# Low-order dense products in bfloat16, sums ordered by operand type, and value products of two heads side by side

## The chip, the core and the metric

The kernel runs on one core of one Trainium2 chip. The metric is the device time of one execution in microseconds, as the median of the runs. TensorE (PE) multiplies, with its weight loads shown apart as PEld; VectorE (DVE), ScalarE (ACT) and GpSimd (POOL) do the elementwise work; SyncE (SP) issues most transfers.

## What is computed

Two layers of a hybrid decoder over 528 tokens (16 learned ones and 512 given) of width 1024, in float32:

```python
for l in range(2):
    u = rmsnorm(h, norm_mix[l])
    proj = u @ w_in[l]                      # 3340 columns
    mix = concat(gated_deltanet(...), diff_attention(...), swa_sinks(...), mamba2_ssd(...))
    h = h + mix @ w_out[l]
    u = rmsnorm(h, norm_ffn[l])
    h = h + (swiglu(u) if l == 0 else moe_swiglu(u))   # dense 2816; top 2 of 8 experts, 3584
y = rmsnorm(h, norm_final)[16:]
```

## The kernel before, in words

Activations lie transposed: 128 features on the partitions, 8 feature blocks, 528 tokens in two halves of 264 columns. A float32 matrix product is made of three cheaper ones. `split` (L192) cuts a float32 tile `raw` in two: `hi` is raw cast to float32r on ACT, `lo` is raw minus hi, also float32r, on DVE, or on POOL where `eng` is 2. `mm3` (L198) then issues hi by hi, hi by low and low by hi into one PSUM bank, 128 by 128 weights against 264 columns each. So a sum over 8 feature blocks is 24 float32r products, and one over 4 blocks (the output projection) 12.

Four stages follow one another. **Mixers 0** (layer 0): `norm` makes `uh` and `ul`; six *early* sums (the small columns and two tiles of keys) run while norm still works; then 24 more weight tiles go through `proj`, each loaded by `loadw` one tile ahead (DMA into `wraw`, two buffers; ACT casts `wh`; POOL subtracts `wl`), each tile as two sums of 24 products in four pieces of 6. Between the pieces run the steps of the four token mixers. Their order on PE is written out by hand: `TURNS` is a string of letters, one per step, p for a piece of projection, x for differential attention, s for sliding window attention, a and b for DeltaNet, d for the state space mixer; each generator's `yield` ends a step. Last comes `outproj` in two halves of 8 tiles. **The dense FFN** of layer 0 (`ffn`): 22 blocks of hidden features, two weight tiles each, then 24 tiles on the way down, all through `mm3`. **Mixers 1** is mixers 0 for layer 1. **The experts** (`up`, `down`): 8 experts with float32r high products and bfloat16 low ones, grouped by type in `mm2`; nothing there is touched.

In differential attention (`diff`, L941), `pv` (L1015) transposes one head's weights (`aT`, and the first 16 keys into the bank of `dpo`), ends the step, and in the next step multiplies them with `V`: 64 output rows, thus half the array's columns, one head after the other. `swa` (L1038) does the same per group (`waT`, `wpo`). These operands are plain float32, and each such product appears as two PE instructions in the trace. All engines but PE take their order from the tile scheduler, and work through it in that order.

Of the kernel before, what the change touches and what calls it, by code (L numbers as in the profile page):

```python
# [181 lines left out]
class Trunk:  # L182
    def __init__(self, tc, A, out, dumps=None):
        self.tc, self.nc, self.A, self.out, self.dumps = tc, tc.nc, A, out, dumps or {}
        self.nlayers = LAYERS
        self.overflow = True

# [122 lines left out]

    def four(self, name, dt=F32):
        return self.eight(name, dt).rearrange("p a b -> p (a b)")[:, :4 * D].rearrange("p (a b) -> p a b", a=4)
# [10 lines left out]
    def norm(self, pool, hT, wcol, l, uh, ul, rsb, t0=0):  # L323
# [3 lines left out]
        for k in range(KT):  # L327
            u = self.ftile("u")
            nc.vector.tensor_scalar(out=u[:, t0:], in0=hT[:, k, t0:], scalar1=self.par[:, l, wcol + k:wcol + k + 1], scalar2=None, op0=ALU.mult)
            self.split(u[:, t0:], uh[:, k, t0:], ul[:, k, t0:])  # L330
# [17 lines left out]
    def _mixers(self, ctx, l, hT):  # L348
# [10 lines left out]
        ul = self.ul = self.eight("ul", F32R)  # L359
# [76 lines left out]
    def mixed(self, name, y):  # L436

        for i in range(2):
            self.dump(f"{name}{self.l}_{i}", y[:, i])
            self.split(y[:, i], self.uh[:, PLACE[name] + i], self.ul[:, PLACE[name] + i])  # L440


    def proj_k(self, k, wh, wl, ps, j):
        s = slice(j * HALF, (j + 1) * HALF)
        self.mm3(ps[:wh.shape[2], :HALF], wh[:, k], wl[:, k], self.uh[:, k, s], self.ul[:, k, s], k == 0, k == KT - 1)

    def proj(self, j, half):
# [3 lines left out]
        for i in range(2):  # L451
            ps = self.ppt("pp")
            for k in range(KT):
                self.proj_k(k, wh, wl, ps, i)
                if k % 2 and k < KT - 1:
                    yield
            half(i, slice(i * HALF, (i + 1) * HALF), ps[:, :HALF])
# [483 lines left out]
    def diff(self):  # L941
# [18 lines left out]
        prev = None  # L960
        for i in range(2):
            yield from self.wait(f"f{i}")
            for c, (t0, n) in reversed(list(enumerate(CH))):
# [16 lines left out]
                for q in range(2):  # L980
# [31 lines left out]
        yield from prev  # L1012
        yield from self.headnorm(self.ma, fq, 4, 1.0 / 64, [dw, dw])

    def pv(self, a, c, h):  # L1015

        nc, tp = self.nc, self.tp
        t0, n = CH[c]
        pt = self.ma("aT", [128, 4, 128])
        at = tp.tile([128, 4, 128], F32, tag="aT", name="aT")  # L1020
        for j in range(1, c + 1):
            nc.tensor.transpose(pt[:, j - 1, :n], a[:n, CH[j][0]:CH[j][0] + 128], self.ident[:n, :n])
        if c:
            nc.scalar.copy(at[:, :c, :n], pt[:, :c, :n])
        po = self.ma("dpo", [128, 2, 128])
        nc.tensor.transpose(po[:16, 1, :n], a[:n, 0:16], self.ident[:n, :n])
        a0 = tp.tile([16, 128], F32, tag="aT0", name="aT0", bufs=1)
        nc.vector.tensor_copy(a0[:, :n], po[:16, 1, :n])
        po = po[:, 0]
        yield  # L1030
        p, vcol = slice(64 * (h % 2), 64 * (h % 2) + 64), 64 * h
        self.mm(po[p, :n], self.V[:16, 0, vcol:vcol + 64], a0[:, :n], True, c == 0)
        for j in range(1, c + 1):
            self.mm(po[p, :n], self.V[:, j, vcol:vcol + 64], at[:, j - 1, :n], False, j == c)

        nc.scalar.copy(self.fqk[p, 0, h // 2, t0:t0 + n], po[p, :n])

    def swa(self):  # L1038
# [4 lines left out]
        for c, (t0, n) in enumerate(CH):  # L1043
# [32 lines left out]
            yield  # L1076
            for g in range(2):
                p = slice(64 * g, 64 * g + 64)
                e = ee[:, 2 * g:2 * g + 2]

                ops = [[], []]
                v = self.V[:, :, 256 + 64 * g:320 + 64 * g]
                if full:
                    pt = self.ma("waT", [128, 2, 2, 128])
                    at = tp.tile([128, 2, 2, 128], F32, tag="waT", name="waT", bufs=1)
                    for r in range(2):
                        for q, j in enumerate(full):
                            k0 = CH[j][0] - s0
                            nc.tensor.transpose(pt[:, r, q, :n], e[:n, r, k0:k0 + 128], self.ident[:n, :n])
                            ops[r].append((v[:, j], at[:, r, q, :n]))  # L1090
                    nc.scalar.copy(at[:, :, :len(full), :n], pt[:, :, :len(full), :n])
                po = self.ma("wpo", [128, 4, 128])
                if c < 2:
                    a0 = tp.tile([16, 2, 128], F32, tag="waT0", name="waT0", bufs=1)
                    for r in range(2):
                        nc.tensor.transpose(po[:16, 2 + r, :n], e[:n, r, 0:16], self.ident[:n, :n])
                        ops[r].append((v[:16, 0], a0[:, r, :n]))
                    nc.vector.tensor_copy(a0[:, :, :n], po[:16, 2:4, :n])
                yield
                for r in range(2):  # L1100
                    for q, (vv, aa) in enumerate(ops[r]):
                        self.mm(po[p, r, :n], vv, aa, q == 0, q == len(ops[r]) - 1)

                nc.scalar.copy(wq[p, :, ts], po[p, 0:2, :n])
                yield
        self.stage.add("sw")

    def outproj(self, half, hT=None):
# [34 lines left out]
        for d in range(KT):  # L1143
# [7 lines left out]
            for j in range(2):  # L1151
                s = slice(w0 + j * hn, w0 + (j + 1) * hn)
                ps = banks[d % len(banks)]("ops")
                for q, k in enumerate(OUTK[half]):
# [546 lines left out]
```

## Time and profile before

| | us |
|---|---|
| median of 3 runs | 2416.12 (2413.11 to 2421.19) |
| the profiled execution | 2410.97 |
| its span, first to last instruction | 2409.1 |
| PE busy | 2320.4 (96%) |
| DVE / ACT / POOL busy | 1690.4 / 1307.9 / 291.8 |

The span is the stretch that all views share; the profiled execution's own time is 1.9 us longer. A busy time is the union of an engine's instructions. Matmuls overlap, so the mean length of one (280 ns and more) is not its price; the distance between the starts of two is. The granted clock is the share of full speed (2.4 GHz) that TensorE was given; it is 2.4 or 1.2 GHz at any moment, and a stage shows the mean.

### The profile page before, as it was taken

How to read it: one execution, taken by the hardware profiler on the slowest of the kernel's cores; microseconds unless marked ns; L12 is line 12 of the kernel's file. 1: busy time of each engine (PE TensorE's matmuls, PEld its weight loads, DVE VectorE, ACT ScalarE, POOL GpSimd, SP SyncE). 2: the span in 40 equal slices, each digit the busy share in tenths (PEclk: the TensorE clock that was granted, in tenths of full speed). 3: DMA queues.
4: the chain of work that ended last, by engine and by line, in shares of the span. 5: the costliest groups of instructions: out<-in, count | busy, mean ns of one | idle time of the engine just before them, and what ended most of it. 6: DMA issues, size and time to landing. Idle time of an engine off the chain costs nothing. (4 is left out here: it accounts for less than half of the span.)

```text
span 2409.1 us, 52816 instructions
## 1 busy us (share of the span) xinstructions
PE 2320.4 (96%) x22285; PEld 2158.4 (90%) x22285; DVE 1690.4 (70%) x2674; ACT 1307.9 (54%) x2004; POOL 291.8 (12%) x186
## 2 busy tenths in 40 slices
PE   7999999999999999999998999999999999999996
PEld 6887778999999987777788999999999999999895
DVE  7655566644433467556555989899998989798896
ACT  4333344333321323334225979787887878676684
POOL 3210112211110022111131300000000000010000
PEclk9999999999999989999898999999999999999998
DMA  4110012222223311001025999989899888888692
GB/s 133 62 37 19 28 49 77 79 88 88 93 88 106 110 53 53 28 27 36 23 89 193 373 377 367 368 350 361 336 361 353 338 333 336 308 351 316 255 365 107
DMA packets 81619, 452.84 MB, mean 188 GB/s; under 512 B 12324, under 2 KB 13236, under 8 KB 38368
## 3 DMA queue, kind: packets, MB, share of 16 engines
q1 hardware_dynamic: 76720, 435.76, 48.7%
q0 software_dynamic: 4656, 13.64, 1.5%
q8 instruction: 177, 2.90, 0.5%
q14 instruction: 66, 0.54, 0.1%
HBM read 439.68 MB, written 9.70 MB: 187 GB/s over the span
## 5 line engine op out<-in xcount | busy, mean ns | idle before, releaser
L190 PE MATMUL gu<-xT,eh 128*128 128x256 f32 (+5 forms) x3584 | 516.1, 296 | 4.0 <-ACT eh L1620 2.3
L190 PEld LDWEIGHTS gu<-xT,eh 128*128 128x128 f32 x3584 | 469.3, 189 | 7.7 <-ACT eh L1620 3.9
L1625 DVE TENSOR_TENSOR el<-erx,eh 128x2048 bf16<-128x2048 f32 x192 | 437.7, 2291 | 40.8 <-ACT eh L1620 38.1
L1620 ACT CAST eh<-erx 128x2048 fp32r<-128x2048 f32 x192 | 365.1, 1909 | 70.5 <-PE gu L190 26.7
L1625 DVE TENSOR_TENSOR el<-er,eh 128x2048 bf16<-128x2048 f32 x144 | 329.7, 2292 | 46.7 <-ACT eh L1620 46.0
L190 PEld LDWEIGHTS <-el 128*128 128x128 bf16 x5376 | 323.5, 97 | 22.6 <-DVE el L1625 1.5
L1620 ACT CAST eh<-er 128x2048 fp32r<-128x2048 f32 x144 | 274.5, 1909 | 52.0 <-PE yacc L190 28.3
L195 ACT CAST wh<-wraw 128x1024 fp32r<-128x1024 f32 (+2 forms) x138 | 141.1, 1024 | 288.0 <-PE dn L190 93.2
L190 PE MATMUL pp<-uh,wh 128*128 128x264 f32 (+1 forms) x864 | 271.7, 315 | 13.5 <-ACT uh L195 7.2
L190 PE MATMUL yacc<-h,eh 128*128 128x256 f32 (+5 forms) x1792 | 259.6, 296 | 0.8 <-ACT eh L1620 0.4
L190 PE MATMUL gu<-xb,el 128*128 128x128 bf16 (+5 forms) x3584 | 256.1, 224 | 0.0
L190 PE MATMUL pp<-uh,wl 128*128 128x264 f32 (+1 forms) x864 | 252.0, 292 | 4.1 <-POOL wl L196 3.5
L190 PE MATMUL pp<-ul,wh 128*128 128x264 f32 (+1 forms) x864 | 252.0, 292 | 1.3 <-DVE ul L196 1.1
L196 POOL TENSOR_TENSOR wl<-wraw,wh 128x1024 fp32r<-128x1024 f32 x66 | 159.7, 2421 | 676.3 <-ACT wh L195 559.5
L190 PEld LDWEIGHTS yacc<-h,eh 128*128 128x128 f32 x1792 | 234.5, 189 | 2.4 <-DVE yT L1676 0.9
L190 PE MATMUL gu<-fuh,wh 128*128 128x264 f32 x704 | 201.9, 287 | 0.0
L190 PE MATMUL gu<-ful,wh 128*128 128x264 f32 x704 | 201.5, 286 | 0.0
L190 PE MATMUL gu<-fuh,wl 128*128 128x264 f32 x704 | 200.6, 285 | 0.0
L190 PEld LDWEIGHTS pp<-uh,wh 128*128 128x128 f32 (+1 forms) x864 | 165.8, 192 | 32.6 <-issue 11.1
L190 PEld LDWEIGHTS pp<-uh,wl 128*128 128x128 f32 (+1 forms) x864 | 165.7, 192 | 6.5 <-POOL wl L196 3.9
L190 PEld LDWEIGHTS pp<-ul,wh 128*128 128x128 f32 (+1 forms) x864 | 166.3, 193 | 3.1 <-DVE ul L196 2.0
L196 DVE TENSOR_TENSOR wl<-wraw,wh 128x1024 fp32r<-128x1024 f32 (+2 forms) x72 | 84.2, 1169 | 94.5 <-ACT wh L195 94.2
(393 smaller groups left out, 3974.1 us busy)
## 6 DMA issues: line engine op xcount, KB each, us to landing
erx<-in_m_gu_dram SPq DMA_DIRECT2D x128, 1024.0 KB, 6.8
er<-in_m_gu_dram SPq DMA_DIRECT2D x96, 1024.0 KB, 7.6
erx<-in_m_d_dram SPq DMA_DIRECT2D x64, 1024.0 KB, 6.9
er<-in_m_d_dram SPq DMA_DIRECT2D x48, 1024.0 KB, 7.6
wraw<-in_w_b_dram SPq DMA_DIRECT2D x52, 512.0 KB, 3.7
wraw<-in_f_gu_dram SPq DMA_DIRECT2D x44, 512.0 KB, 3.7
wraw<-in_w_o_dram SPq DMA_DIRECT2D x16, 512.0 KB, 3.7
wraw<-in_f_d_dram SPq DMA_DIRECT2D x16, 512.0 KB, 3.5
```

The costliest lines, as they stand in the source:

```text
L190: return self.nc.tensor.matmul(out, lhsT, rhs, start=start, stop=stop, skip_group_check=True, **kw)
L195: nc.scalar.copy(hi, raw)
L196: (nc.gpsimd if eng == 2 else nc.vector).tensor_tensor(out=lo, in0=raw, in1=hi, op=ALU.subtract)
L1620: self.lastact = nc.scalar.copy(wh, raw)
L1625: nc.vector.tensor_tensor(out=wl, in0=raw, in1=wh, op=ALU.subtract)
```

## The change

1. A split now yields three tiles: `hi` in float32r as before, `low[0]` = raw minus hi in bfloat16, and `low[1]` = raw cast to bfloat16, a second ACT pass over the same tile. The two bfloat16 tiles take the room of the one float32r tile. Each product hi by low becomes `low[1]` by `low[0]`: of three products per feature block, one stays float32r and two are bfloat16.
2. `mm3s` orders a sum by type: all its float32r products first, then all its bfloat16 ones, and the other way round in the next sum (`turn_hi`), so the type changes once per sum. `proj` still cuts a sum into four pieces of 6; the early sums are grouped per feature block.
3. `pv` waits for two heads and multiplies them by turns, each into its own half of one bank; `swa` does so for its two groups. The number of steps, and `TURNS`, stay as they are. The transposed first 16 keys go into the fourth slot of the `aT` bank (a bank of their own in the last chunk).

```diff
-    def split(self, raw, hi, lo, eng=0):
+    def split(self, raw, hi, low, eng=0):
         nc.scalar.copy(hi, raw)
-        (nc.gpsimd if eng == 2 else nc.vector).tensor_tensor(out=lo, in0=raw, in1=hi, op=ALU.subtract)
+        (nc.gpsimd if eng == 2 else nc.vector).tensor_tensor(out=low[0], in0=raw, in1=hi, op=ALU.subtract)
+        nc.scalar.copy(low[1], raw)

-    def mm3(self, out, ah, al, bh, bl, start, stop):
-        self.mm(out, ah, bh, start, False)
-        self.mm(out, ah, bl, False, False)
-        self.mm(out, al, bh, False, stop)
+    def mm3s(self, out, terms, first=True, last=True, n=0):
+        ops = [[(wh, xh) for wh, _, xh, _ in terms], [p for _, wl, _, xl in terms for p in ((wl[1], xl[0]), (wl[0], xl[1]))]]
+        ops = ops[self.turn_hi] + ops[1 - self.turn_hi]
+        self.turn_hi = 1 - self.turn_hi
+        for i, (w, x) in enumerate(ops):
+            self.mm(out, w, x, first and i == 0, last and i == len(ops) - 1)
+            if n and i % n == n - 1 and i < len(ops) - 1:
+                yield
...
+    def eightb(self, name):
+        return self.b8.tile([128, 2, KT, T], BF16, tag="b8", name=name)
...
-        ul = self.ul = self.eight("ul", F32R)
+        ul = self.ul = self.eightb("ul")
...
         for k in range(KT):
-            for (wh, wl), ps in zip(ahead, early):
-                for j in range(2):
-                    self.proj_k(k, wh, wl, ps[j], j)
+            for part in range(2):
+                for (wh, wl), ps in zip(ahead, early):
+                    for j in range(2):
+                        s, o = slice(j * HALF, (j + 1) * HALF), ps[j][:wh.shape[2], :HALF]
+                        if not part:
+                            self.mm(o, wh[:, k], uh[:, k, s], k == 0, False)
+                        else:
+                            for q in range(2):
+                                self.mm(o, wl[:, 1 - q, k], ul[:, q, k, s], False, k == KT - 1 and q == 1)
...
-            for k in range(KT):
-                self.proj_k(k, wh, wl, ps, i)
-                if k % 2 and k < KT - 1:
-                    yield
+            yield from self.mm3s(ps[:wh.shape[2], :HALF], [(wh[:, k], self.both(wl, k), self.uh[:, k, s], self.both(self.ul, k, s)) for k in range(KT)], n=6)
...
                     if prev:
-                        yield from prev
-                    prev = self.pv(e[:, 1], c, 2 * i + q)
+                        pair.append(self.turn(*prev))
+                        yield
+                        if len(pair) == 2:
+                            self.pv(pair)
+                            pair = []
+                    prev = e[:, 1], c, 2 * i + q
...
+    def pv(self, pair):
+        po = self.ma("dpo", [128, 128])
+        for j in [*range(1, c + 1), 0]:
+            for _, h, a0, at in pair:
+                p, v = slice(64 * (h % 2), 64 * (h % 2) + 64), slice(64 * h, 64 * h + 64)
+                if j:
+                    self.mm(po[p, :n], self.V[:, j, v], at[:, j - 1, :n], j == 1, False)
+                else:
+                    self.mm(po[p, :n], self.V[:16, 0, v], a0[:, :n], c == 0, True)
+        nc.scalar.copy(self.fqk[:, 0, h0 // 2, t0:t0 + n], po[:, :n])
...
+            po = self.ma("wpo", [128, 2, 128])
+            for r in range(2):
+                for q in range(len(ops[0][r])):
+                    for g in range(2):
+                        self.mm(po[64 * g:64 * g + 64, r, :n], *ops[g][r][q], q == 0, q == len(ops[g][r]) - 1)
+            nc.scalar.copy(wq[:, :, ts], po[:, :, :n])
...
-        wl = self.wp.tile([128, KT, 128], F32R, tag="wl", name="wl")
+        wl = self.wp.tile([128, 2, KT, 128], BF16, tag="wl", name="wl")
```

Where it moves instructions. On PE, in the steady dense FFN (`gu` are the gate and up sums, `fuh`, `ful` the split activations), before:

```order
L190 MATMUL gu_5734<-ful_5214,wh_5704 128x264
L190 MATMUL gu_5734<-fuh_5213,wl_5705 128x264
L190 MATMUL gu_5734<-fuh_5213,wh_5704 128x264
L190 MATMUL gu_5734<-ful_5214,wh_5704 128x264
L190 MATMUL gu_5734<-fuh_5213,wl_5705 128x264
L190 MATMUL gu_5765<-fuh_5213,wh_5760 128x264
```

and now, at the boundary of two sums:

```order
L191 LDWEIGHTS wl
L191 MATMUL gu<-ful,wl 128x264
L191 MATMUL gu<-fuh,wh 128x264 x16
L191 LDWEIGHTS wl
L191 MATMUL gu<-ful,wl 128x264
L191 LDWEIGHTS wl
L191 MATMUL gu<-ful,wl 128x264
```

The three kinds no longer alternate: 32 bfloat16 products (two sums' low parts, each with a weight load of its own in the list) stand between 16 float32r ones (two sums' high parts).

On PE, in mixers 0, at the first chunk of differential attention (`fe` the attention weights, `fs` the next scores, `kq` a DeltaNet product, `aT_…` the first 16 keys), before, for one head:

```order
L1022 MATMUL aT<-ident,fe 128x128 x4
L1026 MATMUL dpo<-ident,fe 16x128
...
L190 MATMUL dpo<-aT_1266,V 64x128
L190 MATMUL dpo<-aT,V 64x128 x4
L190 MATMUL fs<-fqk 128x400 x2
```

and now, for the second head and then both:

```order
L1050 MATMUL aT<-ident,fe 128x128 x4
L1052 MATMUL aT_1445<-ident,fe 16x128
...
L191 MATMUL kq<-kbq,knqv 128x256 x4
L191 MATMUL dpo<-aT,V 64x128 x8
L191 MATMUL dpo<-aT_1279,V 64x128
L191 MATMUL dpo<-aT_1439,V 64x128
L191 MATMUL fs<-fqk 128x400 x2
```

The first head's products have moved behind the second head's transposes, and the ten products of two heads stand in one block, head by turn with head.

On ACT, in mixers 0, a little later (`fe` the exponentials of the scores, `dD` those of DeltaNet's decays, `fqk` the copy out of `dpo`), before:

```order
L195 CAST wh<-wraw 128x1024
L677 ACTIVATE dD<-lp,ngc 128x128 x4
L1024 COPY aT<-aT 128x512
L677 ACTIVATE dD<-lp,ngc 16x16 x4
L1036 COPY fqk<-dpo 64x128
L997 ACTIVATE fe,fsm<-fs,fmx 128x400
L195 CAST wh<-wraw 128x1024
```

and now:

```order
L198 CAST wl<-wraw 128x1024
L1026 ACTIVATE fe<-fe,frr 128x400
L196 CAST wh<-wraw 128x1024
L698 ACTIVATE dD<-lp,ngc 128x128 x4
L1054 COPY aT<-aT 128x512
L698 ACTIVATE dD<-lp,ngc 16x16 x4
L1072 COPY fqk<-dpo 128x128
L198 CAST wl<-wraw 128x1024
```

For each weight tile there is a second pass, `wl<-wraw`, and it stands in the same queue, between the same links of the mixers' chains; there are half as many copies out of `dpo`, of twice the rows.

## Rows read from the trace of the kernel before

**Rows 1.** The page: span, and busy time and instructions of each engine.
```profile
span 2409.1 us, 52816 instructions
PE 2320.4 (96%) x22285; PEld 2158.4 (90%) x22285; DVE 1690.4 (70%) x2674; ACT 1307.9 (54%) x2004; POOL 291.8 (12%) x186
```

**Rows 2.** Busy time by stage: mixers 0, dense FFN, mixers 1, experts.
```profile
core 0: us, PE busy (x) PEld busy (x) DVE busy (x) ACT busy (x) POOL busy (x), PEclk, DMA share, GB/s
0.00:442.60 442.60, 412.06 (x3992) 349.97 (x3992) 285.83 (x756) 169.34 (x417) 92.39 (x46) 0.98 0.18 59
442.60:833.50 390.90, 390.75 (x3187) 390.01 (x3186) 155.35 (x253) 108.34 (x169) 48.10 (x44) 0.99 0.30 92
833.50:1309.00 475.50, 442.43 (x4110) 378.99 (x4108) 277.34 (x772) 171.51 (x409) 92.18 (x46) 0.95 0.16 54
1309.00:2409.00 1100.00, 1075.17 (x11000) 1039.46 (x11000) 971.86 (x895) 858.71 (x1011) 59.11 (x50) 0.99 0.86 332
```

**Rows 3.** Groups of PE instructions, 500 to 700 us (steady dense FFN).
```profile
...
L190 PE MATMUL gu<-fuh,wl 128*128 128x264 f32 x548 | 155.3, 283 | 0.0
```

**Rows 4.** Timeline of PE in mixers 0: start, length in us, instruction.
```profile
...
414.02 0.28 PE L190 MATMUL ops<-uh,wl 128*128 128x264 f32 x1
414.24 0.51 PE L190 MATMUL fps<-rw,selb 12*128 12x264 bf16 x3
414.67 0.39 PE L190 MATMUL ops<-uh,wh 128*128 128x264 f32 x1
414.90 0.28 PE L190 MATMUL ops<-ul,wh 128*128 128x264 f32 x1
```

**Rows 5.** The same, where two bf16 forms follow each other.
```profile
...
123.77 0.40 PE L190 MATMUL fps<-rw,selb 48*128 48x264 bf16 x2
124.10 0.39 PE L190 MATMUL lp<-cb,identb 128*128 128x512 bf16 x1
```

**Rows 6.** Timeline of PE in the expert stage, three groups in a row.
```profile
...
1599.81 2.20 PE L190 MATMUL gu<-xT,eh 128*128 128x264 f32 x16
1601.85 1.09 PE L190 MATMUL gu<-xb,el 128*128 128x132 bf16 x16
1602.75 0.49 PE L190 MATMUL gu<-xT,eh 128*128 128x264 f32 x2
```

**Rows 7.** Groups of PE instructions: one kind of dense product per stage, of three.
```profile
...
L190 PE MATMUL pp<-uh,wl 128*128 128x264 f32 (+1 forms) x864 | 252.0, 292 | 4.1 <-POOL wl L196 3.5 <-DVE wl L196 0.6
...
L190 PE MATMUL gu<-fuh,wl 128*128 128x264 f32 x704 | 200.6, 285 | 0.0
...
L190 PE MATMUL dn<-hh,wl 128*128 128x264 f32 x352 | 99.9, 284 | 0.0
...
L190 PE MATMUL ops<-uh,wl 128*128 128x264 f32 (+1 forms) x256 | 72.9, 285 | 0.0
```

**Rows 8.** The same view, products of half the array's columns in two mixers.
```profile
...
L190 PE MATMUL dpo<-aT,V 128*64 128x128 f32 (+2 forms) x232 | 38.8, 293 | 4.5 <-DVE aT L1028 4.5
...
L190 PE MATMUL wpo<-waT,V 128*64 128x128 f32 (+2 forms) x136 | 19.9, 278 | 0.8 <-ACT waT L1091 0.7
```

**Rows 9.** Timeline of PE: half-array products of one head, then of four heads.
```profile
344.06 1.23 PE L190 MATMUL dpo<-aT,V 16*64 16x128 f32 x8 [0.37 <-DVE aT L1028]
...
355.12 0.45 PE L190 MATMUL sy<-sG,xd 128*64 128x128 f32 x4
...
355.82 0.44 PE L190 MATMUL sy<-sCE,sH 128*64 128x128 f32 x4
356.19 0.44 PE L1022 MATMUL aT<-ident,fe 128*128 128x128 f32 x2
```

**Rows 10.** Groups of ACT instructions, 0 to 1309 us: the casts of the splits.
```profile
...
L195 ACT CAST wh<-wraw 128x1024 fp32r<-128x1024 f32 (+2 forms) x138 | 141.1, 1024 | 288.0 <-PE dn L190 93.2 <-PE gu L190 87.4 <-PE pp L190 60.6
...
L195 ACT CAST uh<-u 128x528 fp32r<-128x528 f32 x16 | 9.4, 628 | 5.8 <-DVE u L329 5.8
```

**Rows 11.** What PE waited for, 0 to 1309 us: total us, times, longest.
```profile
...
PE pp L190 <- ACT uh L195: 7.2, 2, 6.9
```

More of the change, by code (lines that the diff above doesn't have):

```diff
@@ L186, in __init__, with mm3 @@
         self.overflow = True
+        self.turn_hi = 0
     def mm(self, out, lhsT, rhs, start, stop, **kw):
         return self.nc.tensor.matmul(out, lhsT, rhs, start=start, stop=stop, skip_group_check=True, **kw)
-    def split(self, raw, hi, lo, eng=0):
+    def split(self, raw, hi, low, eng=0):
         nc = self.nc
         nc.scalar.copy(hi, raw)
-        (nc.gpsimd if eng == 2 else nc.vector).tensor_tensor(out=lo, in0=raw, in1=hi, op=ALU.subtract)
-    def mm3(self, out, ah, al, bh, bl, start, stop):
-        self.mm(out, ah, bh, start, False)
-        self.mm(out, ah, bl, False, False)
-        self.mm(out, al, bh, False, stop)
+        (nc.gpsimd if eng == 2 else nc.vector).tensor_tensor(out=low[0], in0=raw, in1=hi, op=ALU.subtract)
+        nc.scalar.copy(low[1], raw)
+    def mm3(self, out, terms, first=True, last=True):
+        for _ in self.mm3s(out, terms, first, last):
+            pass
+    def mm3s(self, out, terms, first=True, last=True, n=0):
[6 more added lines that the diff above has]
+                yield
     def sums(self, ps_, src, mat, R, scale, pool):
@@ L439, in mixed @@
             self.dump(f"{name}{self.l}_{i}", y[:, i])
[L440 to L445, printed above, removed]
+            self.split(y[:, i], self.uh[:, PLACE[name] + i], self.both(self.ul, PLACE[name] + i))
     def proj(self, j, half):
@@ L959, in diff @@
         fq, fk = self.fqk[:, 0], self.fqk[:, 1]
-        prev = None
+        prev, pair = None, []
         for i in range(2):
@@ L1008, in diff @@
                     if prev:
-                        yield from prev
-                    prev = self.pv(e[:, 1], c, 2 * i + q)
+                        pair.append(self.turn(*prev))
[4 more added lines that the diff above has]
+                    prev = e[:, 1], c, 2 * i + q
         yield
-        yield from prev
+        pair.append(self.turn(*prev))
+        yield
+        self.pv(pair)
@@ L1023, in pv @@
         if c:
             nc.scalar.copy(at[:, :c, :n], pt[:, :c, :n])
[L1025 to L1032, printed above, removed]
@@ L1033, in pv @@
-        for j in range(1, c + 1):
-            self.mm(po[p, :n], self.V[:, j, vcol:vcol + 64], at[:, j - 1, :n], False, j == c)
-        nc.scalar.copy(self.fqk[p, 0, h // 2, t0:t0 + n], po[p, :n])
+        nc.vector.tensor_copy(a0[:, :n], p0[:, :n])
+        return c, h, a0, at
+    def pv(self, pair):
+        nc = self.nc
+        c, h0 = pair[0][:2]
+        t0, n = CH[c]
+        po = self.ma("dpo", [128, 128])
[7 more added lines that the diff above has]
+        nc.scalar.copy(self.fqk[:, 0, h0 // 2, t0:t0 + n], po[:, :n])
@@ L1076, in swa @@
             yield
+            ops = [[[], []], [[], []]]
             for g in range(2):
-                p = slice(64 * g, 64 * g + 64)
                 e = ee[:, 2 * g:2 * g + 2]
-                ops = [[], []]
                 v = self.V[:, :, 256 + 64 * g:320 + 64 * g]
-                if full:
[L1084 to L1090, printed above, removed]
+                pt = self.ma("waT", [128, 2, 2, 128])
+                at = tp.tile([128, 2, 2, 128], F32, tag="waT", name="waT", bufs=2)
+                for r in range(2):
+                    for q, j in enumerate(full):
+                        k0 = CH[j][0] - s0
+                        nc.tensor.transpose(pt[:, r, q, :n], e[:n, r, k0:k0 + 128], self.ident[:n, :n])
+                        ops[g][r].append((v[:, j], at[:, r, q, :n]))
+                    if c < 2:
+                        nc.tensor.transpose(pt[:16, r, 1, :n], e[:n, r, 0:16], self.ident[:n, :n])
+                        ops[g][r].append((v[:16, 0], at[:16, r, 1, :n]))
+                if full:
@@ L1091, in swa @@
                     nc.scalar.copy(at[:, :, :len(full), :n], pt[:, :, :len(full), :n])
-                po = self.ma("wpo", [128, 4, 128])
                 if c < 2:
[L1094 to L1098, printed above, removed]
@@ L1099, in swa @@
-                yield
[L1100 to L1105, printed above, removed]
+                    nc.vector.tensor_copy(at[:16, :, 1, :n], pt[:16, :, 1, :n])
+                yield
+            yield
+            po = self.ma("wpo", [128, 2, 128])
+            for r in range(2):
+                for q in range(len(ops[0][r])):
+                    for g in range(2):
+                        self.mm(po[64 * g:64 * g + 64, r, :n], *ops[g][r][q], q == 0, q == len(ops[g][r]) - 1)
```

35 lines of the change are left out of this document (20 added, 15 removed).

## The prediction

> **What bounds the kernel now.** I read the page first: PE is busy 96% of the span, DVE 70%, ACT 54% [rows 1]. Then the stages, since that mean hides their limits [rows 2]. In the dense FFN (442.6 to 833.5 us) PE is busy 390.75 of 390.90 us, DVE 155 and ACT 108: it lasts as long as its matmuls. In the two mixer stages PE is busy 412 of 442.6 us and 442 of 475.5 us; the 64 us left are waits in chains that run through DVE and ACT, so matmul time saved there comes out only where no chain takes over. The experts (1100 us) are untouched and end what went before, so I count them as unchanged.
>
> The trace counts the dense float32r products by kind: 864 `pp`, 704 `gu`, 352 `dn`, 256 `ops` of one kind, and as many of the two others [rows 7]. Two of three kinds become bfloat16: 2 × 1056 = 2112 in the FFN, 2 × 1120 = 2240 in the mixers, 4352 in all. The sums are 88 + 48 in the FFN (44 tiles up, 24 down, two halves each) and 108 + 64 in the mixers: 308, each with one change of type.
>
> **1. The price of a product.** In steady FFN, 200 us hold 548 float32r products of 264 columns of one kind [rows 3] and 547 of each of the two others, 1642 in all: 121.8 ns each. At 2.4 GHz the 264 columns alone take 110, so at most 12 ns can be won. The nearest bfloat16 rows are two. In the experts, 16 bfloat16 products of 132 columns fill the 0.90 us from 1601.85 to 1602.75 [rows 6]: 56 ns, so 112.5 ns for 264 columns. In mixers 0, three `fps` products of 264 columns span 0.51 us from first start to last end, and their float32r neighbour lasts 0.28 alone [rows 4]: (0.51 − 0.28) / 2 = 115 ns. I take 113, nearer the long steady rows with full weights; ends 112.5 and 115. That saves 8.8 ns (6.8 to 9.3): 18.6 us in the FFN, 19.7 us in the mixers. There the granted clock averages 0.98 and 0.95 [rows 2], which makes about 7% of the time half speed; in that, 264 columns take 220 ns in either type, so I count 18.3.
>
> The Trainium skill, "TensorE: Matmul & The Clock Gate", section on the back-to-back issue gap, gives N/2.4 + 2.5 ns for a warm matmul, with no operand type in it: 112.5 ns at 264 columns. The float32r row (121.8 ns) differs from it, so the row decides; taken for bfloat16 alone it would save 40 us before deductions, where I have 38.
>
> **2. Changes of type.** In the experts, 16 float32r products of 264 columns take 2.04 us up to the first bfloat16 one [rows 6], against 16 × 0.1218 = 1.95: a pair of changes costs 0.09 us there. Here the float32r weights after the last bfloat16 product load beside a product twice as long, so I take half, 0.023 us per change; ends 0 and 0.045. That is 136 × 0.023 = 3.1 us in the FFN and 172 × 0.023 = 4.0 in the mixers.
>
> **3. Two heads side by side.** `dpo` takes 38.8 us for 232 instructions, `wpo` 19.9 for 136 [rows 8]: 58.7 us, all in the mixers, one half of the array idle. What it costs when four heads' products lie in both halves, `sy` shows: 16 instructions, in four groups of 4, between 355.12 and the start of the next work at 356.19 [rows 9]: 67 ns each with the change-over, against 167 for `dpo` (38.8 / 232). At 67 the saving is 58.7 − 368 × 0.067 = 34 us; mere halving gives 29; with a quarter of that lost to groups too short to overlap (the 16-token chunk, two products) 22. I take halving less the half-speed share, 27.
>
> **4. What it adds.** ACT gets 138 further passes over weight tiles at 1.02 us [rows 10] and as many further passes over activations as there are splits. In the FFN that is 68 × 1.0 = 70 us plus some 25 on activations, on top of 108 busy of 391: hidden; if the cover were gone it would show as PE waiting for `wl`. In the mixers it is 70 × 1.02 = 72 us plus 32 passes of 0.63 [rows 10] = 20: 92 us on top of 341 busy of 918 [rows 2]. They stand in ACT's queue between links of the chains; what that costs I put into the share below. Plainly exposed is only the start of a stage, where PE follows `norm` block by block: before, PE waited 7.2 us for `uh` casts, in two places [rows 11]. Eight further passes of 0.63 us in each of three norms are 15 us of ACT time; PE's own work per block (18 products, 2.2 us) covers most, so 3 us; ends 0 and 9. The bfloat16 subtraction writes fewer bytes from the same inputs, and I leave it at its price; weight tiles come a tile ahead, and POOL is busy 92 us per mixer stage [rows 2]. No transfer is added; a `wraw` buffer is held one pass longer, which the tile of lead time covers. The `dpo` copies halve in number.
>
> **Which share comes out.** FFN: 18.6 − 3.1 = 15.5 us, all of it. Mixers: 18.3 − 4.0 + 27 = 41.3 us of PE time; I take three quarters, 31, because PE already stands for 64 of 918 us at ends of chains, where shorter filling work only lengthens the wait, and because the added ACT passes delay some links; ends one half and all. Sum: 15.5 + 31 − 3 = 43.5 us. The profiled execution took 2411.0 us, which gives 2367.5. The median of the runs stands 5 us above it; from there the forecast is 2416 − 43.5 = **2372.5 us**.
>
> **The rivals.**
> *A. A change of type is dear.* Where `fps` (bfloat16) stands between float32r products, the start before it is 0.22 us off instead of 0.12, the one after it about 0.20 instead of 0.11, and the next 0.23 instead of 0.12 [rows 4]: 0.29 us per pair, 0.145 per change. If type alone did that, 308 changes would cost 45 us, and products and changes together would lose 8 us (45 − 36.9). With 27 × 0.75 = 20 from the pairs and 3 lost at the starts: 9 us faster, 2407. Against it: `fps` uses 12 or 48 of 128 rows, and where bfloat16 `fps` is followed by bfloat16 `lp` on 128 rows the gap is the same 0.21 us (second start at 123.77 + 0.40 − 0.28, next at 124.10) [rows 5]; and the experts' change costs 0.045 [rows 6]. So the shape does it. The Trainium skill, "TensorEngine Tiling (Array Packing)", section on key properties, says that changing the tiling mode drains the engine; it does not name the type, and these rows agree.
> *B. The chains hold the mixers.* Only a quarter of the 41.3 us comes out: 15.5 + 10 − 3 = 22.5 us, 2394. For it: chains through DVE and ACT already end 64 us of waits. Against: DVE is busy 60% in the mixers, and most of PE's pieces there are filling work.
> *C. Slower: ACT's queue.* The 92 us of extra passes in the mixers delay exponentials and copies that PE waits for. It decides once 47% of them (43.5 / 92) reach PE's path; at three quarters, 69 us, the time is 2416 − 43.5 + 69 = 2441. For it: the passes stand directly ahead of such links, in order. Against: ACT is idle six tenths of these stages, and in 918 us the longest wait of PE for a cast is 6.9 us, at the very start [rows 11].
> *D. More than forecast.* All of the mixers' 41.3 us comes out, `sy`'s price holds for the pairs (34), changes cost nothing: 18.6 + 18.3 + 34 − 3 = 68 us, 2348.
> That the change does not do what it says is excluded by the instruction order: the products, types and pairs stand there as told.
>
> **How the numbers follow.** Chances: forecast 0.58, A 0.10, B 0.17, C 0.05, D 0.10. The low ends together (115 ns, 0.045 per change, half of the mixers with pairs at 22, 9 us at the starts) leave (14.4 − 6.1) + (14.2 − 7.7 + 22) / 2 − 9 = 13.5 us, 2402; the high ends are D. So 2348 to 2402 holds the forecast, B and half of D, about 0.8. A measurement of this kernel tells 0.3% (7 us) from no change. Faster by more: forecast, B, D and part of A, 0.87; within: the rest of A and a C that just cancels the gain, 0.08; slower: C, 0.05.
>
> **What would show it.** In the changed kernel's profile: the FFN some 375 us long, with bfloat16 products 113 ns apart; `dpo` and `wpo` together near 30 us busy; ACT some 185 us busier before the experts, PE's waits for ACT little longer; both mixer stages 12 to 18 us shorter; the experts within 3 us of 1100. Step 1 is wrong if steady bfloat16 products stand 118 ns or more apart; 2 if the gap at a change of type reaches 0.2 us; 3 if `dpo` stays above 25 us; the share, if the mixers shrink by less than 20 us together. The whole is wrong if the time is above 2402.

## The result, and the profile after

The changed kernel took 2380.68 us in the median of 4 runs (2376.56 to 2388.00), the kernel before, beside it, 2416.40 (4 runs): ratio 0.983, 95% interval 0.980 to 0.986, 36 us less. The forecast was 2372.5 in a range of 2348 to 2402. The profiled execution took 2376.56 us, 34.4 less than that of before.

The page of the changed kernel, against [rows 1]:

```profile
span 2374.8 us, 53054 instructions
PE 2268.1 (96%) x22285; PEld 2023.3 (85%) x22285; DVE 1689.6 (71%) x2674; ACT 1461.9 (62%) x2199; POOL 290.3 (12%) x186
```

PE is busy 52 us less for as many instructions, ACT 154 us more. Then the four stages, cut at the same first instructions as [rows 2] (columns as there):

```profile
0.00:427.50 427.50, 389.87 (x3993) 306.94 (x3993) 284.83 (x755) 208.32 (x460) 89.38 (x46) 0.98 0.19 60
427.50:805.10 377.60, 374.44 (x3188) 337.90 (x3187) 157.04 (x254) 192.74 (x292) 49.82 (x45) 0.98 0.31 97
805.10:1275.70 470.60, 429.72 (x4110) 339.44 (x4107) 276.39 (x773) 202.44 (x439) 91.17 (x46) 0.92 0.17 56
1275.70:2374.80 1099.10, 1074.05 (x11000) 1038.98 (x11000) 971.32 (x895) 858.41 (x1011) 59.96 (x50) 0.99 0.86 332
```

Mixers 0 are 15.1 us shorter, the FFN 13.3, mixers 1 only 4.9, the experts 0.9. The two mixer stages got the same edits; what differs is the granted clock of mixers 1, 0.92 where it was 0.95.

The price of products, by the timeline of steady FFN (start, length in us):

```profile
565.06 2.19 PE L191 MATMUL gu<-fuh,wh 128*128 128x264 f32 x16
567.09 3.77 PE L191 MATMUL gu<-ful,wl 128*128 128x264 bf16 x32
570.62 2.18 PE L191 MATMUL gu<-fuh,wh 128*128 128x264 f32 x16
```

From 565.06 to 570.62, 5.56 us, stand 16 float32r and 32 bfloat16 products and two changes of type. At 121.8 and 112.5 ns the products alone make 5.55: a change costs about 5 ns, an estimate from the last digit.

The pairs (groups of PE instructions) against [rows 8], and ACT's second passes over weight tiles against the first ones in [rows 10]:

```profile
L191 PE MATMUL dpo<-aT,V 128*64 128x128 f32 (+2 forms) x232 | 21.7, 297 | 1.8 <-DVE aT L1055 1.8
L191 PE MATMUL wpo<-waT,V 128*64 128x128 f32 (+2 forms) x136 | 10.0, 279 | 0.0
```

```profile
L198 ACT CAST wl<-wraw 128x1024 bf16<-128x1024 f32 (+2 forms) x138 | 140.8, 1022 | 178.1 <-PE dn L191 65.0 <-issue 39.1 <-PE pp L191 28.0
```

dpo and wpo take 31.7 us where they took 58.7. The second pass costs ACT what the first does, 1022 ns a tile against 1024.

Where the mixers' gain went shows best in one stretch of mixers 1: DeltaNet's last two scans, from `pS` to the last `po`, with the same products in both kernels. Busy time by stretch, before and after:

```profile
1156.50:1165.60 9.10, 9.10 (x73) 6.01 (x72) 3.69 (x6) 2.35 (x6) 0.67 (x1) 1.00 0.20 59
```

```profile
1117.20:1131.90 14.70, 14.70 (x72) 8.53 (x71) 2.09 (x5) 2.35 (x6) 0.00 (x0) 0.54 0.09 32
```

73 and 72 PE instructions, busy throughout, in 9.1 us at full clock and in 14.7 us at 0.54 of it. Up to the experts the records put TensorE at 1.2 GHz for 72 us before and 110 after, of them 48 and 76 in mixers 1 and 5 and 14 in the FFN. PE also waits a little more: the waits view to 1320 us sums to 65 us before and 81 after.

### The profile page after: what moved, and what is told of

It reads as the page before. It is cut to its first block, busy times and chain, and to the rows that moved or that the text cites. A ratio compares the mean times of both kernels' runs of the same rounds, so it can differ in the third digit from the quotient of the medians.

```text
span 2374.8 us, 53054 instructions
## 1 busy us (share of the span) xinstructions
PE 2268.1 (96%) x22285; PEld 2023.3 (85%) x22285; DVE 1689.6 (71%) x2674; ACT 1461.9 (62%) x2199; POOL 290.3 (12%) x186
## 5 line engine op out<-in xcount | busy, mean ns | idle before, releaser
L191 PEld LDWEIGHTS <-wl 128*128 128x128 bf16 (+1 forms) x4352 | 412.8, 100 | 100.1 <-issue 20.4
L191 PE MATMUL pp<-ul,wl 128*128 128x264 bf16 (+1 forms) x1728 | 244.9, 289 | 8.6 <-DVE xp L507 3.0
L198 ACT CAST wl<-wraw 128x1024 bf16<-128x1024 f32 (+2 forms) x138 | 140.8, 1022 | 178.1 <-PE dn L191 65.0
L197 POOL TENSOR_TENSOR wl<-wraw,wh 128x1024 bf16<-128x1024 f32 x66 | 158.1, 2396 | 664.5 <-ACT wh L196 523.9
L191 PE MATMUL gu<-ful,wl 128*128 128x264 bf16 x1408 | 170.1, 280 | 0.0
L196 ACT CAST wh<-wraw 128x1024 fp32r<-128x1024 f32 (+2 forms) x138 | 140.9, 1022 | 28.1 <-PE pp L191 20.1
L191 PE MATMUL pp<-uh,wh 128*128 128x264 f32 (+1 forms) x864 | 147.3, 306 | 10.6 <-ACT uh L196 7.2
L197 DVE TENSOR_TENSOR wl<-wraw,wh 128x1024 bf16<-128x1024 f32 (+2 forms) x72 | 84.1, 1168 | 99.2 <-ACT wh L196 99.2
L191 PE MATMUL yacc<-hb,el 128*128 128x128 bf16 (+5 forms) x1792 | 129.2, 223 | 0.5 <-DVE el L1659 0.4
L1683 ACT COPY gt<-gu 128x256 f32<-128x256 f32 (+5 forms) x224 | 86.0, 384 | 29.6 <-PE gu L191 26.2
L191 PE MATMUL gu<-fuh,wh 128*128 128x264 f32 x704 | 98.1, 291 | 3.2 <-ACT fuh L196 3.2
```

The lines of the kernel that those rows point to most:

```text
L191: return self.nc.tensor.matmul(out, lhsT, rhs, start=start, stop=stop, skip_group_check=True, **kw)
L197: (nc.gpsimd if eng == 2 else nc.vector).tensor_tensor(out=low[0], in0=raw, in1=hi, op=ALU.subtract)
L198: nc.scalar.copy(low[1], raw)
L1683: nc.scalar.copy(t[:, :, j], ps[:, :, C:2 * C])
```

## The experiments

Eleven kernels and the changed one once more ran on four chips, those of one group on one chip (the weight view alone on the fourth), each group beside 11 runs of the kernel before. Since the runs of one kernel differ by up to 30 us and follow their granted clock, I take a second reading besides the ratio. A run's time at 1.2 GHz is 2 × (1 − mean granted clock) × its time. Over the 117 runs whose clock is known, time = a constant of the kernel + 0.40 × time at 1.2 GHz, with a standard deviation of 1.5 us. The constant, *at full clock* below, is an estimate of what the kernel would take at 2.4 GHz throughout; that of the kernel before came out at 2372.9 to 2373.4 on four chips. No run had less than 96 us at 1.2 GHz, so the constant itself lies outside what was measured. The difference of two constants is firmer: it says how far two kernels lie apart at equal time at 1.2 GHz. The same 0.40, taken off single stages of a profile, is good to 2 or 3 us only: the FFN, the same code in both, comes to 372 us in the changed kernel and to 369.5 in bf16 and order only.

| kernel | runs | median, us | ratio to before | at 1.2 GHz, mean us | at full clock, us |
|---|---|---|---|---|---|
| before | 44 | 2422 to 2429 per chip | 1 | 132 | 2373 |
| changed, first | 4 | 2380.7 | 0.983 (0.980 to 0.986) | 144 | 2324 |
| changed, again | 6 | 2386.3 | 0.982 (0.978 to 0.987) | 161 | 2323 |
| pairs only | 4 | 2407.1 | 0.992 (0.989 to 0.995) | 136 | 2353 |
| bf16 and order only | 4 | 2396.8 | 0.988 (0.985 to 0.990) | 130 | 2346 |
| order per block | 8 | 2408.9 | 0.994 (0.991 to 0.996) | 154 | 2348 |
| no second pass | 4 | 2374.0 | 0.979 (0.977 to 0.981) | 148 | 2315 |
| stepped views | 6 | 2385.9 | 0.981 (0.977 to 0.986) | 156 | 2324 |
| pieces moved | 6 | 2375.2 | 0.978 (0.974 to 0.983) | 137 | 2322 |
| po by turns | 6 | 2365.5 | 0.973 (0.968 to 0.977) | 132 | 2311 |
| both edits | 6 | 2357.6 | 0.972 (0.968 to 0.975) | 119 | 2311 |
| both, POOL pass | 6 | 2368.8 | 0.977 (0.973 to 0.981) | 137 | 2314 |
| both, FFN start | 6 | 2358.1 | 0.971 (0.968 to 0.975) | 121 | 2311 |
| both, weight view | 6 | 2356.0 | 0.974 (0.970 to 0.977) | 123 | 2309 |

At full clock the change is worth 50 us. The changed kernel spends 12 to 29 us more at 1.2 GHz on average (144 and 161 against 132), which takes 5 to 12 of them back; on one chip it was 161 against 141.

**The parts alone.** Pairs only is the kernel before with `turn`, the paired `pv` and the paired `swa` of the change; the other is the changed kernel with the old ones:

```diff
 # pairs only, against before
-                    prev = self.pv(e[:, 1], c, 2 * i + q)
+                        pair.append(self.turn(*prev))
...
 # bf16 and order only, against the changed kernel
-                        pair.append(self.turn(*prev))
+                    prev = self.pv(e[:, 1], c, 2 * i + q)
```

> The kernel before with part 3 alone: value products of two heads (two groups) side by side, all dense products float32r as before. My theory (the parts add, a part of the mixers' gain is held back by waits): dpo + wpo fall from 58.7 to about 32 us of PE time, FFN unchanged at 391 us; of the 27 us saved half to all comes out, so 2389 to 2403 us, near 2396 (ratio 0.992). Rival B (chains hold the mixers): PE time falls as much, but the mixer stages shrink by less than 8 us together, 2408 or more. Rival of the half-speed clock: the waits that replace PE work bring more time at 1.2 GHz than the 72 us of the kernel before.

> The changed kernel without part 3: bfloat16 low products and sums ordered by type, value products one head at a time as before. My theory: FFN steady part -19 us and its start +3, mixers 0 and 1 up to -18 less what the starts lose (+6 and +2), so 2384 to 2398, near 2391 (ratio 0.989); with the first experiment's gain it should add up to the 36 us of the whole change within 6 us. Rival B: mixers together shrink by less than 4 us, total 2400. If the two parts alone give much more than 36 us together, they take the same waits' room in the mixers.

Measured: 0.992 and 0.988, the ratios expected (0.992 and 0.989). The pairs' median of 2407.1 us misses the 2389 to 2403 put down for it, beside a kernel before that took 2425 on this chip. At full clock the two save 20.6 and 26.7 us, together 47 of the 50: the parts add. Both rivals B looked at the length of the mixer stages. In the profiles these are 2.6 and 17 us longer together than before, each with some 56 us more of half speed; at equal clock they are some 20 and 5 us shorter. So it is the clock that hides the pairs' gain, while bfloat16 and order brought little there: some 20 of their 26.7 us came in the FFN. In the profiles the pairs' kernel has FFN 390.5 us, as before, and mixers 1 of 481.8 us, 6 *longer* than before, with 92 us of them at 1.2 GHz; the other has FFN 370.9. The stretch of the last two scans, in the pairs' kernel and in the one without pairs:

```profile
1149.80:1163.50 13.70, 13.70 (x73) 8.52 (x71) 2.21 (x5) 2.35 (x6) 0.00 (x0) 0.60 0.12 39
```

```profile
1155.30:1164.40 9.10, 9.10 (x73) 5.72 (x69) 3.47 (x6) 2.41 (x7) 0.46 (x1) 1.00 0.18 59
```

So the half speed in this place comes with the pairs, not with bfloat16. It is there as well in the profiles of the next two kernels, which have pairs. Over whole runs the pairs alone add little half speed that can be seen: 136 us on average, against 131 in the kernel before on this chip and 130 without pairs, while the runs of one kernel lie up to 70 us apart in it.

**The order of a sum.**

```diff
-        ops = [[(wh, xh) for wh, _, xh, _ in terms], [p for _, wl, _, xl in terms for p in ((wl[1], xl[0]), (wl[0], xl[1]))]]
-        ops = ops[self.turn_hi] + ops[1 - self.turn_hi]
-        self.turn_hi = 1 - self.turn_hi
+        ops = [p for wh, wl, xh, xl in terms for p in ((wh, xh), (wl[1], xl[0]), (wl[0], xl[1]))]
```

> The changed kernel with the order of a sum back at one feature block after the other (float32r, bfloat16, bfloat16), so the type changes twice per block instead of once per sum: 2176 pairs of changes. My theory: a pair costs about 14 ns as at the sums' boundaries in the trace of the changed kernel (248 ns for two products in one direction, 234 in the other), so at most 2176 x 0.014 = 30 us, 15 of it in the FFN (375 becomes about 390), less 5 to 8 us that the starts get back since each block is wanted one at a time: 2385 to 2405 us. Rival A (a type change is dear, 0.046 us or more each): FFN's 1056 pairs add 97 us or more, total near 2580. Third possibility: changes free and the order by type only hurts the starts: 2372 to 2376.

Measured: 0.994; at full clock 24 us slower than the changed kernel. (The median of 2408.9 lies above the 2385 to 2405 expected, which started from the first measurement's 2381.) The way down of the FFN, 352 triples, in the kernel before, per block and by type:

```profile
704.80:833.50 128.70, 128.70 (x1058) 128.70 (x1057) 40.94 (x55) 26.89 (x32) 0.00 (x0) 1.00 0.33 98
```

```profile
690.30:817.30 127.00, 127.00 (x1055) 106.85 (x1053) 40.23 (x55) 50.90 (x64) 0.00 (x0) 1.00 0.32 99
```

```profile
682.70:804.90 122.20, 122.20 (x1057) 110.94 (x1056) 40.21 (x55) 52.01 (x65) 0.00 (x0) 1.00 0.35 103
```

Between the last two, 4.8 us are 14 ns a pair of changes, as expected; rival A's price would have made 32 or more. But 14 ns is most of the 19 that two bfloat16 products save. Against float32r alone, bfloat16 without the order by type won 1.7 us of 6.5. The starts got something back, as expected: PE's waits sum to 70 us against 81, and 24 us were lost of the 30 that 2176 pairs make.

**The second ACT pass left out.** Raw in bfloat16 is replaced by the low tile, so the kernel leaves out the two products of hi by low and puts low by low in their place.

```diff
-        nc.scalar.copy(low[1], raw)
...
-        return t[:, 0, k, s], t[:, 1, k, s]
+        return t[:, 0, k, s], t[:, 0, k, s]
```

> The changed kernel without the second ACT pass: the product's second bfloat16 operand is the low tile itself, so raw is never cast to bfloat16, and the two low products of a pair are low by low (their number, type and order as in the changed kernel). ACT loses some 154 us of work before the experts. My theory: these passes make PE wait at the starts (outproj half 0, FFN, mixers 1) and in the chains that run through ACT: the time falls by 8 to 15 us against the changed kernel, to 2366 to 2373, outproj half 0 from 49 back to about 43 us, the FFN's start from 24.4 to about 21 us, mixers 1 shorter by 3 to 8. Rival: ACT has room for them (62% busy) and the losses come of the order by type and the clock alone: within 3 us of the changed kernel.

Measured: 0.979, 8 to 9 us less than the changed kernel at full clock, the size expected (the median of 2374.0 lies 1 us above the range). The reason given isn't borne out, though. PE's waits for casts at the output projections of both layers are as long without the passes (its waits view, first the changed kernel):

```profile
PE ops L191 <- ACT uh L196: 9.8, 3, 5.5
```

```profile
PE ops L191 <- ACT uh L196: 9.9, 3, 6.0
```

All waits of PE sum to 75 us here, against 81 with the passes; of what fell, 3.2 us were waits for the norm's casts at the FFN's start. That start, its first 96 products, took 15.7 us here and 22.0 in the changed kernel. But it took 15.3 in bf16 and order only, which has the passes: what the two short ones share is the clock, 3 to 4 us at 1.2 GHz against 14. At equal clock, then, the passes cost the FFN nothing (371.4 us without them, 370.9 in bf16 and order only, one profile each), and the 8 us lie in the mixers, at no place that these profiles show.

**Three edits beside the changed kernel.** First, views instead of passes: where raw in bfloat16 is wanted, the upper half of each word of the float32r tile is read.

```diff
+    def top(hi):
+        return hi.bitcast(BF16).rearrange("p (n two) -> p n two", two=2)[:, :, 1]
...
-        nc.scalar.copy(low[1], raw)
...
-((wl[1], xl[0]), (wl[0], xl[1]))
+((self.top(wh), xl), (wl, self.top(xh)))
```

> The changed kernel itself, once more, beside the three below: 0.983 of the kernel before, within the interval of its first measurement (0.980 to 0.986).

> The changed kernel without the second ACT pass: where a product wants raw in bfloat16, it reads the upper half of each 4-byte word of the float32r tile (a bfloat16 view with a step of two), so hi truncated stands for raw rounded. My theory of the sums of parts: if such an operand streams and loads like a packed one (112 to 113 ns apart), this is worth what leaving the pass out was worth, about 9 us against the changed kernel at the same clock (2372 if that is 2381; ratio to before 0.979). Rival: a stepped operand costs TensorE what a float32 one does, 121.8 ns, or more: then each of the 2176 products with a stepped activation, or weight, gives 9 ns back, 20 us a side, and it is 10 to 30 us slower than the changed kernel.

Measured: the changed kernel again at 0.982; the views at 0.981, and at full clock no gain. The timeline of the FFN's way down, eleven pairs of products apart:

```profile
720.74 0.29 PE L191 MATMUL dn<-hl,wh 128*128 128x264 bf16 x1
...
723.28 0.27 PE L191 MATMUL dn<-hl,wh 128*128 128x264 bf16 x1
```

A pair takes 2.54 / 11 = 0.231 us, where two packed ones take 0.225. By the starts in the records (328 of each kind) the next product starts 111.7 ns after one with a stepped weight (`hl,wh`) and 118.1 after one with a stepped activation (`hh,wl`). The rival was right on one side: 2176 stepped activations × 5.6 ns = 12 us, against the 8 that the missing passes gave.

Second, two pieces of projection moved in mixers 1, from behind DeltaNet's last scans to between them:

```diff
 # part of the second string of TURNS
-pbbbppxpxxaxbabpaxpdppddpdpxpx
+pbbbppxpxxapxbabppaxdpddpdpxpx
```

> The changed kernel with two pieces of projection moved in the hand-written order of mixers 1: from behind the narrow products of DeltaNet's last two scans (po, pv, rpt) to between them. In the profiles of all four kernels with the products side by side this stretch of some 20 us ran at 1.2 GHz (po at 84 to 100% half speed in the second scan), in the two without them at 2.4. Theory of the clock (what stands before and in the stretch is too little work on TensorE): with two pieces of wide products in it, it runs at 2.4 GHz at least in part, half-speed time in mixers 1 falls by 10 to 20 us and the time by 4 to 8 us. Rival: the half speed comes of the mean load over mixers 1 or falls by chance: the stretch is slow as before, or another is, and the time stays within 2 us at the same total of half-speed time.

Measured: 0.978 beside 0.982; medians 11 us apart, 24 us less at 1.2 GHz on average (12 of them in mixers 1, by the two profiles), at full clock the same (2322 to 2323). The stretch, with six more wide products in it:

```profile
1116.80:1126.40 9.60, 9.60 (x78) 6.13 (x77) 2.58 (x6) 2.35 (x6) 0.00 (x0) 1.00 0.16 55
```

No work was taken away or added, and the stretch that took 14.7 us takes 9.6. That agrees with the theory of the clock. The intervals of the two ratios overlap, so the size of its gain is less certain than its place.

Third, `po` by turns:

```diff
-            for h, p, i in H:
+            for g in (H[:2], H[2:]):
                 if S is not None:
-                    self.mm(po[p, i, :n], S[p, i, :], qg[p, i, ts], True, False)
-                self.mm(po[p, i, :n], vn[:n, h, :], AT[:n, h, :n], S is None, True)
+                    for h, p, i in g:
+                        self.mm(po[p, i, :n], S[p, i, :], qg[p, i, ts], True, False)
+                for h, p, i in g:
+                    self.mm(po[p, i, :n], vn[:n, h, :], AT[:n, h, :n], S is None, True)
```

> The changed kernel with DeltaNet's output products (po, 136 instructions, 31.5 us busy, 0.18 us each at full speed) issued two heads by turns, each in its own half of the array's columns, as the change does with dpo and wpo. If the price of part 3 holds here, 31.5 falls to 16 to 20 us and 6 to 12 us come out at the same clock. Theory of the clock: less work for TensorE in the narrow stretch brings no less half-speed time than the changed kernel has, so the time falls by 3 to 10 us. Rival: the products wait for their weights or for each other, not for columns: po stays above 27 us, time within 2 us.

Measured: 0.973, and 12 us less at full clock. The median fell by 21, more than the 3 to 10 expected, since the time at 1.2 GHz fell too, from 161 to 132 us on average: against the theory, less work in the narrow stretch went with less half speed. Groups of PE instructions, first the changed kernel:

```profile
L191 PE MATMUL po<-dAT,vn 128*64 128x128 f32 (+1 forms) x72 | 16.0, 316 | 0.0
L191 PE MATMUL po<-knqv,dS 64*64 64x128 f32 x64 | 15.5, 327 | 0.0
```

```profile
L191 PE MATMUL po<-dAT,vn 128*64 128x128 f32 (+1 forms) x72 | 8.2, 312 | 0.0
L191 PE MATMUL po<-knqv,dS 64*64 64x128 f32 x64 | 7.5, 313 | 0.0
```

31.5 us became 15.7. Step 3 of the prediction holds for a third product.

**Both edits, and three tries on top.** Both edits is pieces moved and po by turns joined. The tries are:

```diff
 # POOL pass
-        nc.scalar.copy(low[1], raw)
+        nc.gpsimd.tensor_copy(low[1], raw) if eng == 2 else nc.scalar.copy(low[1], raw)
 # FFN start, first block only
-                    self.mm3(ps[:, :HALF], terms)
+            for k in () if f else range(KT):
+                for ps, terms in late:
+                    self.mm(ps[:, :HALF], terms[k][0], terms[k][2], k == 0, False)
...
 # weight view
-((wl[1], xl[0]), (wl[0], xl[1]))
+((self.top(wh), xl[0]), (wl, xl[1]))
```

> The changed kernel with both of the last two edits: two pieces of projection moved into the narrow stretch, and po two heads by turns. From the runs so far each us at 1.2 GHz costs 0.4 us, and at 2.4 GHz throughout the changed kernel would take 2323 us, with po by turns 2312, with the moved pieces 2323. If the two are independent: 2311 at full clock, with 115 to 135 us at half speed 2357 to 2364, ratio to before 0.970 to 0.972. Rival: po by turns has made the stretch so short that the moved pieces no longer matter, same as po by turns alone (132 us of half speed, 2364), or the moved pieces are missed behind the stretch and half speed only moves there.

> The kernel with both edits, and the second pass over the weight tiles of the mixers and output projections on POOL instead of ACT (the activations' and the FFN's stay on ACT). Leaving the second pass out altogether was worth 8 us at full clock. My theory: POOL has room (290 us busy of 2375), the tile is loaded one ahead, so most of it comes out: 3 to 8 us less than the kernel with both edits at the same half-speed time. Rival: POOL's queue now holds two passes of some 2.4 us for each tile, the low tile or its partner comes late, PE waits for POOL at the head of a tile, and the time is the same or up to 10 us longer.

> The kernel with both edits, and the FFN's first block ordered feature block by feature block over its four sums (four float32r products, then eight bfloat16 ones, per block), as the early sums of the mixers are; all other sums by type as in the change. Theory: in the FFN's first 20 us PE waits for one activation block after another since a sum starts with all eight high products; with work for each block as it comes, the half-speed time at the FFN's start (7 to 14 us in the profiles of the changed kernel and its variants) falls to 0 to 4 us and the stage shrinks by 2 to 5 us. Rival: the norm's ACT passes alone set that start: within 1.5 us of the kernel with both edits at the same half-speed time.

> The kernel with both edits (pieces moved, po two heads by turns), in which the weights' bfloat16 operand is the stepped view of the float32r tile, and the activations' stays a packed tile made by the second ACT pass. In the profile of the kernel with both operands stepped, a product with a stepped weight stood 112 ns from the next, one with a stepped activation 118. Theory: the stepped weight is free, so the 138 second passes over weight tiles (141 us of ACT) go at no price: of the 8 us that leaving all second passes out was worth, 4 to 8 come out at equal clock against the kernel with both edits (2311 at 2.4 GHz throughout becomes 2303 to 2307), ratio to before 0.966 to 0.971. Rival: the gain of leaving the passes out was made by the activations' passes, which stand directly before the stages' first products and in the chains; then it is within 2 us of the kernel with both edits at equal clock.

Measured: both edits 0.972, 2357.6 us, 2311 at full clock, 119 us at 1.2 GHz; within what was expected. By the ratio, both edits can't be told from po by turns alone (0.973). Beside the kernel before on its own chip, the one spent 14 us less at 1.2 GHz and the other 8. That the moved pieces still pay on top shows in the stretch of the last scans, which po by turns alone ran in 9.5 us at 0.57 of full clock, and not in the time. The stretch now:

```profile
1113.20:1120.10 6.90, 6.90 (x80) 4.82 (x79) 2.50 (x6) 2.49 (x7) 0.00 (x0) 1.00 0.19 68
```

The POOL pass lost, 3.4 us at full clock. POOL's own row is cheap:

```profile
L198 POOL CAST wl<-wraw 128x1024 bf16<-128x1024 f32 x66 | 74.1, 1125 | 448.6 <-issue 427.3 <-PE pp L191 18.2 <-PE ops L191 3.0
```

but PE's waits rose from 82 to 87 us; only 2.6 of them are for POOL's `wl`, so how the rest comes about stays open. The other order at the FFN's start brought nothing (2311 at full clock, 13.7 us at 1.2 GHz in that stage in both profiles), as the rival said. That the norm's casts set this start isn't shown by it: with the same casts, bf16 and order only ran it in 15.3 us (465.7 to 481.0, clock 0.89) and the changed kernel in 22.0 (427.5 to 449.5, clock 0.69). What decides between the two stays open. The weight view took 130 us off ACT and 2 us off the time at full clock, where 4 to 8 were expected: the rival's bound. So the passes over weights cost almost nothing, and the 8 us of the passes left out must lie elsewhere: in the activations' passes, by elimination only, since no kernel left out those alone.

Both edits beats the kernel before and the changed one, with intervals that don't touch theirs; the FFN start and the weight view are no better within theirs.

## Why the prediction was right, and where a term was off

**Step 1, the price of a product: right.** 112 to 113 ns for bfloat16 against 121.8 was taken as 113, and the FFN's way down won 6.5 us on 704 products, 9.2 ns each. The Trainium skill's formula ("TensorE: Matmul & The Clock Gate", section on the back-to-back issue gap) gives 112.5 ns for 264 columns: the rows agree for bfloat16 and not for float32r.

**Step 2, changes of type: taken too dear.** 0.023 us each stood in the sum; the period of 5.56 us gives 0.005, the kernel ordered per block 0.007. That is 5 us of 308 changes. Part of it was the reading of [rows 6]: the 2.04 us begin at a start that the records put early. In the changed FFN, too, 16 float32r products take 2.03 us up to the first bfloat16 one, 0.08 more than 16 × 0.1218, and the 32 bfloat16 products behind them take 3.53, 0.07 less than 32 × 0.1125. Only a whole period gives the price of a change. Rival A fell. What the step didn't say is that the order earns most of step 1: with a pair of changes per block, 14 of the 19 ns saved would be gone.

**Step 3, two heads side by side: right**, 27.0 us of PE time for 27 taken. Of it 20.6 came out at full clock (pairs only), 0.76, the three quarters that the step on the share took.

**Step 4, ACT: right in load, wrong in place.** The second passes sum to 183 us, 141 on weights and 42 on activations, as forecast; ACT's busy time grew by 154, since the union counts overlapping instructions once and the pairs save copies (9 us, pairs only). At full clock the passes cost 8 us in all; 3 were put at the starts, which the kernel without the passes neither shows nor rules out.

**The share of the mixers: the term that was mis-sized.** It was three quarters, 31 us. The two stages shrank by 15.1 + 4.9 = 20.0, just at the bound given, and mixers 1 missed the "12 to 18". Taking 0.40 us off for each us at 1.2 GHz in the two profiles (19.3 and 20.5 in mixers 0, 47.8 and 75.6 in mixers 1), they shrank by 15.6 and 16.0: 31.6, as forecast. The FFN comes to 17.0 by the same reckoning, for 15.5. So the share at full clock was right as a whole, though not part by part: the pairs gave 0.76 of their 27 us, bfloat16 and order alone some 5 to 7 of the 14.3 put down for them in the mixers. What is missing is a term the sum didn't have: the clock. The prediction took the half-speed time of the kernel before as given. With two heads' products side by side, the narrow DeltaNet products behind them ran at 1.2 GHz, in all seven profiles with pairs and without moved pieces; how the pairs bring that about is not shown. Rival B foresaw a smaller gain in the mixers, but by waits: those grew by 16 us in all (in the profiles they come with bfloat16 and order, 82 us alone, not with the pairs, 68), and at full clock the mixers gave what was forecast.

**Rival C**: the passes cost 8 us at full clock, in the FFN and the mixers together, where 47% of 92 would have had to reach PE's path. **Rival D** lay at 68 us; at full clock the change brought 50.

In the first measurement the kernel before took 2416 us, by its constant (2416 − 2373) / 0.40 = 108 us of them at 1.2 GHz, and the changed kernel 144 us. The 36 us between cost 14 of the 50, and leave the 36 measured, 7.5 short of the forecast. That the forecast came so close is in part luck, in two ways. The sum was 6.5 us too low at full clock, mostly by the price of changes and the 3 us at the starts, and the clock took back 14. And the 108 us of the kernel before are at the low end of its runs (132 on average in the 44 later ones), so how much of the 14 is the change's own doing stays open.

## What to carry to other kernels

A type that makes products cheaper pays only if the products of one type stand together; price the changes against the saving per product, not against the product. Small products that use half the array's columns are worth issuing two by turns into both halves: three kinds of them halved here. When PE work is taken out of a stretch of narrow products, look at the granted clock there in the new profile, and move wide products that are due anyway into it; here the stretch then ran at full clock in four profiles of five.

## What the runs showed that was not expected

- The clock is part of the price of an edit: products in the same stretch took 9.1 us or 14.7 by what stood around them. In the seven profiles with pairs and without moved pieces it ran at 0.52 to 0.60 of full speed, in the two without pairs at 1.00. It is not a rule without exceptions: in one of the five kernels with moved pieces (FFN start) the second scan ran half at 1.2 GHz again.
- A weight read with a step of two costs nothing (111.7 ns to the next product), an activation read so about 6 ns of 112.
- One us at 1.2 GHz costs 0.40 us over all runs, not the 0.5 that fully busy PE would give. Taken kernel by kernel it is 0.41 to 0.43 in the four sets of the kernel before, and 0.17 to 0.48 in the others, which have 4 to 8 runs each; so the 0.40 is a mean, not a constant of the chip.
